# Conv row factors from fp32 sums beside the last input units, the samples' cast queued behind the second key block's, and another order of the last units

## The chip, the cores and the metric

The kernel runs on one core of one Trainium2 chip. The metric is the device time of one execution in microseconds; the time of a kernel is the median of several executions. Engines are named as the profile names them: PE (TensorE, matrix products; PEld its weight loads), DVE (VectorE), ACT (ScalarE), POOL (GpSimd) and SP (SyncE, which here issues the DMAs).

## What is computed

One streaming step of one hybrid layer, for 512 frames of a new stream (the prompt) and 64 frames of a running one (the samples, with 512 cached frames). D is 2048, there are 8 heads of 128, 1024 conv channels in 8 groups, and an FFN of width 5632.

```python
hn = rmsnorm(x, g_norm1)
q, k, v, gb, gc, hc = split(hn @ w_in)              # six blocks of 1024 columns
q = rmsnorm(q, g_q); k = rmsnorm(k, g_k)            # per head
o_attn = stick_breaking_blocks(q, k_all, v_all)     # keys and values: cached + new
u = gc * hc
o_conv = gb * conv3_causal(u)                       # three taps, state from conv_past
mix = concat([rmsnorm(o_attn, g_attn_out), rmsnorm(o_conv, g_conv_out)])   # each over its 1024 channels
x = x + mix @ w_out
h2 = rmsnorm(x, g_norm2)
x = x + (silu(h2 @ w_gate) * (h2 @ w_up)) @ w_down
```

In stick-breaking attention the weight of key s for query t is beta_ts times the product of (1 - beta_tj) over the keys j between them, beta being the sigmoid of the scaled score. Outputs are the new x of both streams, the new key and value rows, and the conv states.

## The kernel before

**Layout.** Frames lie along the free axis: 576 columns (512 prompt frames, then 64 sample frames), handled as two halves of 288 (`HALVES`). Channels lie on the 128 partitions. A product in high precision is made of three fp32r matmuls: an operand is split into a high part (an ACT cast to fp32r) and a low part (a DVE subtraction), and hi·hi, lo·hi and hi·lo are added up in PSUM. `split()` (L230 to L232) does one such split; `whl` tiles hold the split weights.

**Units.** The input projection runs in 22 units (`HEADS_A`, numbered -22 to -1), each two blocks of 128 columns by two halves of frames, made by seven products (1 to 7, a Strassen-like scheme) in place of eight. The last three are -3 (a pair of `gb` groups), -2 (q and k of head 7) and -1 (v of heads 6 and 7). `order` lists all products `(unit, product)`; `run()` issues one, 24 matmuls in eight steps with a `pipe.tick()` behind each. Behind product number k_, `prepare()` splits the operand of number k_ + 4. Products 1, 6, 5 and 3 of a unit add to one bank (`psy`), 7 and 4 to another (`psw`); `kept()` copies psy into a one-buffer tile (tags "ms", "t", "acc") between them, since several results are made of more than one product. `a_done()` finishes a quarter of a unit: for q and k it multiplies by the row factor R1 of the first norm, squares, splits the squares (`s2`) and spawns `normed()`.

**Pipeline.** `Pipeline` is a queue of generators on a count of ticks. What a generator issues between two yields stands in program order at the tick at which it came due; `yield n` puts it off by n ticks, and `spawn(gen, delay)` starts it. `normed()` sums the squares over the partitions with `channel_sums()` (two matmuls with a matrix of ones, into one of two PSUM banks of tag "misc"), forms 1/sqrt with Ln, Exp and a Newton step, and scales q or k. `tokens()` transposes a block on PE (also into "misc" banks) and stores its rows.

**Orders.** PE runs in program order (it is scheduled by hand). For the other engines and the DMA queue, the order of the stage around the change is laid out by a planner at compile time, which takes ready instructions by program order. Each engine then runs its own order and waits on semaphores.

**Conv group and output projection.** A `gb` unit leaves the conv half of `mix` (without its row factor) in `mixc_dram`, and adds the squares to `accc`. Behind the last unit, `group_scale(accc, Rc)` splits the sums of squares, adds them over the partitions with `channel_sums()`, and turns them into row factors `Rc` by `rsqrt_mean()`. `out_proj()` multiplies the conv half by `w_out`, 16 column blocks by two halves of frames; a DVE step (L1005) scales each bank by the row factor and another (L1006) adds it to x.

**Heads.** `heads()` spawns `attend(h)` every 29 ticks, so that the eight heads run beside the conv half's projection. `attend` makes the scores of three query-key groups z2, z1, z0 and of the samples (`zs`), softplus of each, then, by sums with triangular matrices on PE, the exponents; `weights(b)` masks (L1135, DVE), exponentiates (L1137, ACT) and splits (`ph`, `pl`). `po` (L1170, L1173) is the product with the values. For the samples, `sp` (softplus) gets running sums on POOL (L1113 to L1117), `split(sph, spl, sp)` splits it, and `sample_weights()` (L1125 to L1131) uses it later, between the first and the second key block of `po`. The squares of the attention output are added to `accA`, and at the start of the second `out_proj()` the same `group_scale()` gives `Ra`. Then come the FFN's units.

Of the kernel before, what the change touches and what calls it, by code (L numbers as in the profile page):

```python
# [10 lines left out]
F32 = mybir.dt.float32  # L11
F32R = mybir.dt.float32r
AF = mybir.ActivationFunctionType
ALU = mybir.AluOpType
PSUM = bass.MemoryType.PSUM

P = 128
TP = 512
TS = 64
T = TP + TS  # L20
HALF = T // 2
HALVES = ((0, HALF), (HALF, T))
# [79 lines left out]
def tile_hybrid_stream_step(  # L102
# [6 lines left out]
    nc = tc.nc  # L109
    mm = nc.tensor.matmul  # L110
# [5 lines left out]
    kp, vp, ks, vs = k_prompt[0, 0], v_prompt[0, 0], k_sample[0, 0], v_sample[0, 0]  # L116
# [6 lines left out]
    rpool = ctx.enter_context(tc.tile_pool(name="rpool", bufs=1, side="left"))  # L123
    tmp = tc.alloc_tile_pool(name="tmpa", bufs=2, side="left")
# [15 lines left out]
    def misc(name):  # L140
        return ps_z.tile([P, 512], F32, tag="misc", name=name, bufs=2)
# [42 lines left out]
    def load_weight():  # L184
        i = len(raws)
        raws[i], raw3, src = weight_raw(i)
        nc.sync.dma_start(out=raw3, in_=src)
# [33 lines left out]
    pipe = Pipeline()  # L221
# [6 lines left out]
            pipe.tick()  # L228

    def split(hi, lo, src, lo_eng=None):  # L230
        nc.scalar.copy(out=hi, in_=src)  # L231
        (lo_eng or nc.vector).tensor_tensor(out=lo, in0=src, in1=hi.bitcast(F32), op=ALU.subtract)  # L232

    def parts(name, bufs=2):
        t = tmp.tile([P, 2, HALF], F32R, tag="hl", name=name, bufs=bufs)
# [5 lines left out]
    oner = const.tile([P, P], F32R, name="oner")  # L241
# [24 lines left out]
    epsc = const.tile([P, 1], F32, name="epsc")  # L266
# [5 lines left out]
    def rsqrt_mean(dst, src, n, width):  # L272
        ms = tmp.tile([P, HALF], F32, tag="ms", name="ms", bufs=1)[:, :width]
        y = tmp.tile([P, HALF], F32, tag="acc", name="y", bufs=1)[:, :width]
        t = tmp.tile([P, HALF], F32, tag="t", name="t", bufs=1)[:, :width]
        nc.vector.tensor_scalar(out=ms, in0=src, scalar1=1.0 / n, scalar2=EPS, op0=ALU.mult, op1=ALU.add)
        nc.scalar.activation(out=y, in_=ms, func=AF.Ln)
        nc.scalar.activation(out=y, in_=y, func=AF.Exp, scale=-0.5)
        nc.vector.tensor_tensor(out=t, in0=y, in1=y, op=ALU.mult)
        nc.vector.scalar_tensor_tensor(out=t, in0=t, scalar=-0.5, in1=ms, op0=ALU.mult, op1=ALU.mult)  # L280
        nc.vector.scalar_tensor_tensor(out=dst, in0=t, scalar=1.5, in1=y, op0=ALU.add, op1=ALU.mult)

    def channel_sums(src_hi, src_lo, a, b, name):
        ps = misc(name)[:, : b - a]
        mm(ps, oner, src_hi, start=True, stop=False)
        mm(ps, oner, src_lo, start=False, stop=True)
        return ps
# [466 lines left out]
    def tokens(E, dst, dst_s, dram, lag):  # L754
        yield lag
        pa = misc("tok_a")
        for i in range(4):
            nc.tensor.transpose(pa[:, i * P : (i + 1) * P], E[:, i * P : (i + 1) * P], ident)
        ta = hl_tile("tok")[:, :TP]
        nc.scalar.copy(out=ta, in_=pa)  # L760
        ta = ta.rearrange("p (i d) -> p i d", d=P)
        nc.sync.dma_start(out=dst.rearrange("(i p) d -> p i d", p=P), in_=ta)
        if dram is not None:
            nc.sync.dma_start(out=dram[:, :4, :], in_=ta)
        yield 3
        pb = misc("tok_b")
        nc.tensor.transpose(pb[:, :P], E[:, T - P : T], ident)
        tb = hl_tile("tokz")[:, :P]
        nc.scalar.copy(out=tb, in_=pb[:, :P])
        nc.sync.dma_start(out=dst_s, in_=tb[TS:, :])  # L770
        if dram is not None:
            nc.sync.dma_start(out=dram[:, 4, :], in_=tb)
# [3 lines left out]
    accc = []  # L776
# [3 lines left out]
        return ((a, min(b, TP), 0),) + (((TP, b, 2),) if b > TP else ())  # L780

    def normed(n, h, c, a, b, s2, E):
        yield 17
        ms = ss = channel_sums(s2[:, 0], s2[:, 1], a, b, "ss")
        yt = hl_tile("yt")
        y, t = yt[:, :HALF], yt[:, HALF:]
        nc.scalar.activation(out=ms, in_=ss, func=AF.Identity, scale=1.0 / P, bias=epsc)
        nc.scalar.activation(out=y, in_=ms, func=AF.Ln)
        nc.scalar.activation(out=y, in_=y, func=AF.Exp, scale=-0.5)
        nc.scalar.activation(out=t, in_=y, func=AF.Square)  # L790
        nc.vector.scalar_tensor_tensor(out=t, in0=t, scalar=-0.5, in1=ms, op0=ALU.mult, op1=ALU.mult)
        nc.vector.scalar_tensor_tensor(out=t, in0=t, scalar=1.5, in1=y, op0=ALU.add, op1=ALU.mult)
        nc.vector.scalar_tensor_tensor(out=E[:, a:b], in0=E[:, a:b], scalar=col("gk") if c else gqs, in1=t,
                                       op0=ALU.mult, op1=ALU.mult)
        seen[n, c] = seen.get((n, c), 0) + 1
        if seen[n, c] == 2:
            nc.sync.dma_start(out=qk_dram[h, c], in_=E)
            if c:
                pipe.spawn(tokens(E, kp[:, h, :], ks[:, h, :], None, 8 if n == -2 else 20))

    def a_finish(n, c, i, ps, part):
        if UNITS[n][0] == "gb" and c == i == 0:
# [106 lines left out]
             (2 - NA, 5)]  # L909
    for n in range(2 - NA, -3):  # L910
        order += [(n + 1, 1), (n, 3), (n, 4), (n + 1, 2), (n + 1, 6), (n + 1, 7), (n + 1, 5)]
    order += [(-2, 1), (-3, 3), (-3, 4), (-2, 2), (-2, 6), (-2, 5), (-1, 1), (-2, 3), (-1, 2), (-2, 7),
              (-2, 4), (-1, 3), (-1, 6), (-1, 5), (-1, 7), (-1, 4)]
    early = {-NA, 1 - NA, -1}
    mixc = []
    for k_ in range(2, 4):
        prepare(*order[k_])
    for k_, (n, p_) in enumerate(order):
        run(n, p_, n in early)
        if k_ + 4 < len(order):  # L920
            prepare(*order[k_ + 4])
            if order[k_ + 4] in ((-2, 3), (-1, 6)):
                load_weight()
        if (n, p_) == (-1, 3):
            xpool.release()
            cpool = tc.alloc_tile_pool(name="cpool", bufs=1, reuse_waits="tile", side="right")
            mixc = cpool.tile([P, NG, 2, T], F32R, name="mixc")
            for g in range(NG):
                nc.sync.dma_start(out=mixc[:, g].bitcast(F32), in_=mixc_dram[g])
        if (n, p_) == (-1, 7):  # L930
            split_weight(nc.vector)
# [56 lines left out]
    mixa = []  # L988
# [7 lines left out]
    def out_proj(frame, R, after=None):  # L996
        for c in range(D // 256):
            whi, wlo = next_weight()
            load_x2()
            for j in range(2):  # L1000
                kt = 2 * c + j
                for a, b in HALVES:
                    ps = ps_pj.tile([P, HALF], F32, tag="pj", name="pjo")
                    product(ps, whi, wlo, slice(j * P, (j + 1) * P), frame, 8, a, b)
                    nc.vector.tensor_tensor(out=ps, in0=ps, in1=R[:, a:b], op=ALU.mult)  # L1005
                    nc.vector.tensor_tensor(out=x2(kt)[:, a:b], in0=ps, in1=x2(kt)[:, a:b], op=ALU.add)  # L1006
                if after:
                    after(kt)

    Rc = rpool.tile([P, T], F32, tag="R", name="Rc", bufs=2)  # L1010

    def group_scale(acc_, R, bufs):
        p_ = []
        for a, b in HALVES:
            s2 = tmp.tile([P, 2, HALF], F32R, tag="hl", name="s2g", bufs=bufs)
            split(s2[:, 0], s2[:, 1], acc_[:, a:b])
            p_.append(s2)
        yield 4
        for s2, (a, b) in zip(p_, HALVES):
            ss = channel_sums(s2[:, 0], s2[:, 1], a, b, "ssg")  # L1020
            rsqrt_mean(R[:, a:b], ss, 8 * P, HALF)

    def state_out():
        yield 9
# [45 lines left out]
    def attend(h):  # L1070
# [45 lines left out]
        for b in (2, 1, 0):  # L1116
            nc.gpsimd.tensor_tensor(out=sums[:, b * TS : (b + 1) * TS], in0=sums[:, (b + 1) * TS : (b + 2) * TS],  # L1117
                                    in1=sp[:, (b + 1) * TS : (b + 2) * TS], op=ALU.add)
        split(sph, spl, sp)
        yield 8  # L1120
        if h + 1 < NH:
            keys_cached(h + 1)
# [10 lines left out]
        def weights(b):  # L1133
            for i in ((2, 3) if b == 2 else (b,)):
                nc.vector.scalar_tensor_tensor(out=zb[i][:, :P], in0=zb[i][:, :P], scalar=0.0, in1=mneg,  # L1135
                                               op0=ALU.min, op1=ALU.add)
            nc.scalar.activation(out=pr[b][:, : full[b]], in_=z[b][:, : full[b]], func=AF.Exp)  # L1137
            split(ph[b], pl[b], pr[b][:, : width[b]])

        yield 3  # L1140
        mm(zb[3], trif, pb[3], stop=False, **kw)
# [6 lines left out]
        mm(zb[1], trir, pl[1], stop=False, **kw)  # L1148
        mm(zb[1][:, P:], neg1r, s1h, stop=False, **kw)
        mm(zb[1][:, P:], neg1r, s1l, stop=True, **kw)  # L1150
        weights(1)
        yield 4
        mm(zb[0], trir, ph[0], stop=False, **kw)
        mm(zb[0], trir, pl[0], stop=False, **kw)
# [50 lines left out]
            pipe.spawn(attend(h))  # L1205
            yield PERIOD

    pipe.spawn(group_scale(accc[0], Rc, 3))
    pipe.spawn(state_out())
    pipe.spawn(heads())  # L1210
    out_proj(lambda k: (mixc[:, k, 0, :], mixc[:, k, 1, :]), Rc)
    pipe.flush()
    accA = bt["accA"]
    cpool.release()
# [2 lines left out]
    tmp = tc.alloc_tile_pool(name="tmp", bufs=2, reuse_waits="tile", side="left")  # L1217
    lpad = tc.alloc_tile_pool(name="lpad", bufs=1, side="left")
    lpad.tile([P, 64], F32, name="lpad_t")
    Ra = rpool.tile([P, T], F32, tag="R", name="Ra", bufs=2)  # L1220
    pipe.spawn(group_scale(accA, Ra, 2))

# [34 lines left out]
            for k in (4 * m, 4 * m + 2):  # L1259
                nc.sync.dma_start(out=x2_dram[k : k + 2].rearrange("k p t -> p k t"), in_=x2t[k // 2])  # L1260

    out_proj(lambda k: mixa[k], Ra, after_b2)
    R2 = rpool.tile([P, T], F32, tag="R", name="R2", bufs=2)
    parts2 = []
    for i in range(2):
# [340 lines left out]
```

## Time and profile before

| | us |
|---|---|
| median of 3 runs (lowest, highest) | 2406.14 (2406.02, 2406.74) |
| the profiled execution | 2408.49 |
| its span, first to last instruction | 2406.8 |
| PE busy | 2355.5 |
| DVE busy | 1939.7 |
| ACT busy | 1235.0 |
| POOL busy | 298.9 |
| input units | up to about 598 of the span |
| conv projection with the heads | about 598 to 799 |
| attention projection, FFN | from about 799 |

How to read the lines: a row of the timeline has the start, the duration, engine, source line, operation, output<-inputs, shapes and a count, and in brackets the idle time of the engine before it and what ended that. A row of the waits has who waited for whom, the total, the times and the longest. A row of the windows has the stretch and its length, then the busy time (and instructions) of PE, PEld, DVE, ACT and POOL in it, the granted clock of PE, the DMA share and GB/s.

### The profile page before, as it was taken

Reading aid. Unit: us, or ns where it says so; the run is one execution under the profiler, and the core shown is the slowest. Engines: PE = TensorE matmul, PEld = TensorE weight load, DVE = VectorE, ACT = ScalarE, POOL = GpSimd, SP = SyncE. Lnnn points to the kernel's source line nnn. Section 1 sums busy time; section 2 is a strip of 40 time slices with the busy share of each in tenths; the row PEclk is TensorE's granted clock in tenths of the full one; section 3 lists DMA queues with packets and bytes.
Section 4 is the critical chain, followed back from the end, with each engine's and each line's share of the span. In section 5 each row is a group of like instructions: output and inputs, shape, how many; then the busy total and the mean of one; then the engine's idle time right before and its main releaser. Section 6 shows DMA issues by size and latency. Waiting matters only on the chain.

```text
span 2406.8 us, 43812 instructions
## 1 busy us (share of the span) xinstructions
PE 2355.5 (98%) x17609; PEld 2339.5 (97%) x17609; DVE 1939.7 (81%) x2840; ACT 1235.0 (51%) x2207; POOL 298.9 (12%) x377
## 2 busy tenths in 40 slices
PE   8899999999999999999999999999999899999998
PEld 8899999998889999999999999999999899999998
DVE  7888898797677768888888888888888778887875
ACT  7456656455677545444444444444444444444454
POOL 0111121120233222000000000000000002431211
PEclk9999999999999999999999999999999999999999
DMA  7433342535632233535444444444444936885642
GB/s 253 140 113 108 108 140 86 161 99 184 224 107 89 100 127 118 155 112 158 150 128 145 146 143 132 144 150 141 129 152 141 339 112 205 221 226 195 205 128 79
DMA packets 474900, 360.60 MB, mean 150 GB/s; under 512 B 11278, under 2 KB 460680, under 8 KB 474696
## 3 DMA queue, kind: packets, MB, share of 16 engines
q1 hardware_dynamic: 469528, 351.02, 45.7%
q0 software_dynamic: 5168, 6.79, 1.6%
q8 instruction: 138, 2.26, 0.4%
q14 instruction: 66, 0.54, 0.1%
HBM read 281.39 MB, written 76.37 MB: 149 GB/s over the span
## 4 chain that ended last, share of the span: by engine, by line
PE 82%; DVE 6%; ACT 4%; issue 2%; POOL 2%; DMA 1%; SPq 0%; ACTq 0%; DVEq 0%; POOLq 0%
PE psy L405 43%; PE psw L405 21%; PE psx L405 10%; PE pjo L227 5%; DVE whl L232 1%; ACT whl L231 1%; PE pw L1388 1%; ACT ph L231 0%; PE psv L405 0%; PE pot L1511 0%; DVE c L866 0%; DVE raw_b L349 0%; POOL hbl L1117 0%; DMA raw_a<-in_w_down_dram 0%; DVE wlo L180 0%
## 5 line engine op out<-in xcount | busy, mean ns | idle before, releaser
L232 DVE TENSOR_TENSOR whl<-raw_a,whl 128x1024 fp32r<-128x1024 f32 (+4 forms) x376 | 426.4, 1135 | 69.4 <-ACT whl L231 67.8
L405 PE MATMUL psy<-t,whl 128*128 128x288 f32 x2916 | 438.4, 295 | 0.5 <-ACT part L428 0.5
L231 ACT CAST whl<-raw_a 128x1024 fp32r<-128x1024 f32 (+4 forms) x376 | 352.6, 938 | 137.9 <-PE psx L405 47.8
L405 PE MATMUL psy<-h_s,whl 128*128 128x288 f32 x2724 | 411.7, 295 | 6.8 <-ACT part L428 6.8
L405 PEld LDWEIGHTS psy<-t,whl 128*128 128x128 f32 x2916 | 403.7, 189 | 0.9 <-ACT part L428 0.7
L405 PEld LDWEIGHTS psy<-h_s,whl 128*128 128x128 f32 x2724 | 378.5, 189 | 7.3 <-ACT part L428 7.3
L405 PE MATMUL psw<-t,whl 128*128 128x288 f32 x2592 | 377.1, 295 | 0.0
L405 PEld LDWEIGHTS psw<-t,whl 128*128 128x128 f32 x2592 | 354.4, 189 | 0.2
L232 DVE TENSOR_TENSOR whl<-raw_b,whl 128x1024 fp32r<-128x1024 f32 (+5 forms) x230 | 248.7, 1081 | 86.4 <-ACT whl L231 85.1
L231 ACT CAST whl<-raw_b 128x1024 fp32r<-128x1024 f32 (+5 forms) x230 | 207.6, 904 | 206.9 <-PE psw L405 70.8
L428 ACT COPY part<-psy 128x288 f32<-128x288 f32 x303 | 121.2, 400 | 348.5 <-PE psy L405 346.4
L405 PE MATMUL psx<-h_s,whl 128*128 128x288 f32 x1122 | 165.1, 295 | 2.7 <-DVE gs L1368 2.7
L405 PEld LDWEIGHTS psx<-h_s,whl 128*128 128x128 f32 x1122 | 154.1, 188 | 2.9 <-issue 2.9
L231 ACT CAST whl<-s 128x1024 fp32r<-128x1024 f32 (+5 forms) x101 | 93.4, 924 | 119.9 <-PE psw L405 112.3
L405 PE MATMUL psy<-t12a,whl 128*128 128x288 f32 x1056 | 150.5, 295 | 3.1 <-ACT part L428 3.1
L405 PE MATMUL psw<-t34a,whl 128*128 128x288 f32 x1056 | 150.4, 295 | 2.1 <-DVE ghs L854 0.9
L405 PEld LDWEIGHTS psy<-t12a,whl 128*128 128x128 f32 x1056 | 143.5, 188 | 4.0 <-ACT part L428 4.0
L405 PEld LDWEIGHTS psw<-t34a,whl 128*128 128x128 f32 x1056 | 143.2, 188 | 2.7 <-DVE ghs L854 1.1
L227 PE MATMUL pjo<-mixc,whi 128*128 128x288 f32 x512 | 123.0, 307 | 1.2 <-ACT kcT L1063 1.2
L232 DVE TENSOR_TENSOR whl<-s,whl 128x1024 fp32r<-128x1024 f32 (+5 forms) x101 | 107.5, 1064 | 19.6 <-ACT whl L231 18.0
L1331 POOL DMA_DIRECT2D hid_dram<-form x3 | 2.4, 809 | 921.1 <-DVE form L232 921.1
L227 PE MATMUL pjo<-mixa,whi 128*128 128x288 f32 x512 | 102.1, 295 | 0.0
(599 smaller groups left out, 4146.8 us busy)
## 6 DMA issues: line engine op xcount, KB each, us to landing
hid_dram<-form SPq DMA_DIRECT2D x147, 288.0 KB, 2.3
raw_a<-in_w_gate_dram SPq DMA_DIRECT2D x23, 1024.0 KB, 6.2
raw_a<-in_w_up_dram SPq DMA_DIRECT2D x23, 1024.0 KB, 5.5
raw_a<-in_w_in_dram SPq DMA_DIRECT2D x22, 1024.0 KB, 5.5
raw_b<-in_w_in_dram SPq DMA_DIRECT2D x22, 1024.0 KB, 7.9
raw_b<-in_w_gate_dram SPq DMA_DIRECT2D x21, 1024.0 KB, 6.6
raw_b<-in_w_up_dram SPq DMA_DIRECT2D x21, 1024.0 KB, 7.7
h_s<-hid_dram SPq DMA_DIRECT2D x10, 2016.0 KB, 9.2
```

What stands on the lines that cost most here:

```text
L227: mm(ps, w_[:, k, csl], x_[:, a:b], start=(k == 0 and n == 0), stop=(k == nk - 1 and n == 2))
L231: nc.scalar.copy(out=hi, in_=src)
L232: (lo_eng or nc.vector).tensor_tensor(out=lo, in0=src, in1=hi.bitcast(F32), op=ALU.subtract)
L405: mm(ps, whl[:, w_, j, :], x_, start=(start and j == 0 and q == 0), stop=(j == len(xs_) - 1 and q == 2), skip_group_check=True)
L428: nc.scalar.copy(out=t, in_=st["y"])
L1331: q.dma_start(out=hid_dram[fp][2 * n - 2 : 2 * n].rearrange("f p t -> p f t"), in_=t.bitcast(F32))
L1388: mm(pss[j, i], w_[:, k, j * P : (j + 1) * P], x_, start=(kk == 0 and k == 0 and n == 0), stop=(kk == 1 and k == 7 and n == 2))
```

## The change

Four things are changed.

1. `group_scale()` no longer splits the sums of squares. It adds them over the partitions with one fp32 matmul a half, works in place in the PSUM bank and in a tile of tag "hl", and writes the row factors over the sums (`accc`, `accA`), so that `Rc` and `Ra` are gone. One half is done per tick.
2. For the conv half it is spawned behind product (-2, 6) with a delay of 5 ticks, in place of behind the last unit; for the attention half, with a delay of 4.
3. In the order of the last products, (-1, 1) and (-1, 2) come earlier, and (-2, 4) later. For unit -2, `normed()` waits 12 ticks and not 17, and `tokens()` of its keys 5 and not 8. The loads tied to places in the order go with them: two of `w_out`, and those of `mixc` behind (-1, 3).
4. The split of the samples' softplus is traced behind `weights(1)`, and its cast is put behind that call's cast in ACT's order (`tc.issue_after`).

```diff
     def split(hi, lo, src, lo_eng=None):
-        nc.scalar.copy(out=hi, in_=src)
+        cast = nc.scalar.copy(out=hi, in_=src)
         (lo_eng or nc.vector).tensor_tensor(out=lo, in0=src, in1=hi.bitcast(F32), op=ALU.subtract)
+        return cast.ins
...
     def normed(n, h, c, a, b, s2, E):
-        yield 17
+        yield 12 if n == -2 else 17
...
-                pipe.spawn(tokens(E, kp[:, h, :], ks[:, h, :], None, 8 if n == -2 else 20))
+                pipe.spawn(tokens(E, kp[:, h, :], ks[:, h, :], None, 5 if n == -2 else 20))
+
+    def group_scale(acc_, bufs):
+        for a, b in HALVES:
+            ss = misc("ssg")[:, :HALF]
+            mm(ss, oner.bitcast(F32), acc_[:, a:b], start=True, stop=True)
+            yt = tmp.tile([P, 2, HALF], F32, tag="hl", name="ytg", bufs=bufs)
+            y, t = yt[:, 0], yt[:, 1]
+            nc.scalar.activation(out=ss, in_=ss, func=AF.Identity, scale=1.0 / (8 * P), bias=epsc)
+            nc.scalar.activation(out=y, in_=ss, func=AF.Ln)
+            nc.scalar.activation(out=y, in_=y, func=AF.Exp, scale=-0.5)
+            nc.scalar.activation(out=t, in_=y, func=AF.Square)
+            nc.vector.scalar_tensor_tensor(out=t, in0=t, scalar=-0.5, in1=ss, op0=ALU.mult, op1=ALU.mult)
+            nc.vector.scalar_tensor_tensor(out=acc_[:, a:b], in0=t, scalar=1.5, in1=y, op0=ALU.add, op1=ALU.mult)
+            yield 1
...
-    order += [(-2, 1), (-3, 3), (-3, 4), (-2, 2), (-2, 6), (-2, 5), (-1, 1), (-2, 3), (-1, 2), (-2, 7),
-              (-2, 4), (-1, 3), (-1, 6), (-1, 5), (-1, 7), (-1, 4)]
+    order += [(-2, 1), (-3, 3), (-3, 4), (-2, 2), (-2, 6), (-1, 1), (-2, 5), (-1, 2), (-2, 3), (-2, 7), (-1, 3),
+              (-1, 6), (-2, 4), (-1, 5), (-1, 7), (-1, 4)]
...
+        if (n, p_) == (-2, 6):
+            pipe.spawn(group_scale(accc[0], 3), 5)
...
-    Rc = rpool.tile([P, T], F32, tag="R", name="Rc", bufs=2)
-
-    def group_scale(acc_, R, bufs):
-        p_ = []
-        for a, b in HALVES:
-            s2 = tmp.tile([P, 2, HALF], F32R, tag="hl", name="s2g", bufs=bufs)
-            split(s2[:, 0], s2[:, 1], acc_[:, a:b])
-            p_.append(s2)
-        yield 4
-        for s2, (a, b) in zip(p_, HALVES):
-            ss = channel_sums(s2[:, 0], s2[:, 1], a, b, "ssg")
-            rsqrt_mean(R[:, a:b], ss, 8 * P, HALF)
...
-        split(sph, spl, sp)
         yield 8
...
-            split(ph[b], pl[b], pr[b][:, : width[b]])
+            return split(ph[b], pl[b], pr[b][:, : width[b]])
...
-        weights(1)
+        behind = weights(1)
+        with tc.issue_after(behind):
+            split(sph, spl, sp)
...
-    pipe.spawn(group_scale(accc[0], Rc, 3))
...
-    out_proj(lambda k: (mixc[:, k, 0, :], mixc[:, k, 1, :]), Rc)
+    out_proj(lambda k: (mixc[:, k, 0, :], mixc[:, k, 1, :]), accc[0])
...
-    pipe.spawn(group_scale(accA, Ra, 2))
+    pipe.spawn(group_scale(accA, 2), 4)
...
-    out_proj(lambda k: mixa[k], Ra, after_b2)
+    out_proj(lambda k: mixa[k], accA, after_b2)
```

More of the change, by code (lines that the diff above doesn't have):

```diff
@@ L1219, in tile_hybrid_stream_step @@
     lpad.tile([P, 64], F32, name="lpad_t")
-    Ra = rpool.tile([P, T], F32, tag="R", name="Ra", bufs=2)
-    pipe.spawn(group_scale(accA, Ra, 2))
+    pipe.spawn(group_scale(accA, 2), 4)
     h2pool = tc.alloc_tile_pool(name="h2pool", bufs=1, reuse_waits="tile", side="left")
```

## The prediction

> **What bounds the kernel now.** I read the page first, then the busy time by stage, then what PE waited for, and last the order of time around each wait.
>
> ```profile
> span 2406.8 us, 43812 instructions
> PE 2355.5 (98%) x17609; PEld 2339.5 (97%) x17609; DVE 1939.7 (81%) x2840; ACT 1235.0 (51%) x2207; POOL 298.9 (12%) x377
> 549.77:598.13 48.36, 44.75 (x332) 43.61 (x330) 33.46 (x49) 26.13 (x46) 1.78 (x3) 1.00 0.51 183
> 598.13:609.56 11.43, 8.44 (x49) 7.53 (x47) 9.03 (x22) 6.74 (x16) 1.47 (x2) 0.85 0.65 203
> 609.56:799.07 189.51, 178.40 (x1247) 170.85 (x1246) 131.76 (x283) 135.05 (x307) 55.63 (x104) 0.97 0.39 129
> ```
>
> PE is the bound: 2355.5 of 2406.8 us. The three windows are the stages that the diff touches: the last twelve products of the input units, the start of the conv half's output projection, and the eight attention heads beside it. In them PE stands idle 3.61, 2.99 and 11.11 us, 17.7 together, and in two the granted clock is below 1 (0.85, 0.97). So the change can move little more than these waits and the slow stretches behind them; shorter work on DVE or ACT counts only where PE waits for it. PE runs in program order; the other engines' orders come from a planner, so they may shift.
>
> ```profile
> PE po L1170 <- ACT pr L1137: 5.3, 4, 2.5
> PE z L1147 <- ACT ph L231: 2.5, 1, 2.5
> PE pjo L227 <- ACT kcT L1063: 1.2, 1, 1.2
> ACT sph L231 <- POOL hbl L1117: 16.6, 8, 2.9
> ```
>
> Among the heads, PE waits above all for the exponentials of L1137, and ACT itself stands 16.6 us in front of one cast, the samples' sph, until POOL has its sums.
>
> **The change part by part.** Gains carry a minus.
>
> *(a) The last input units.* One product and the waits:
>
> ```profile
> 549.64 3.33 PE L405 MATMUL psx<-bod,whl 128*128 128x288 f32 x24
> 552.81 3.33 PE L405 MATMUL psy<-t12a,whl 128*128 128x288 f32 x24
> 557.78 3.47 PE L405 MATMUL psy<-t12a,whl 128*128 128x288 f32 x24 [1.63 <-ACT part L428]
> 574.88 1.05 PE L405 MATMUL psw<-t34a,whl 128*128 128x288 f32 x6 [0.64 <-DVE E L820]
> 585.74 1.06 PE L405 MATMUL psy<-t12a,whl 128*128 128x288 f32 x6 [0.49 <-ACT part L428]
> ```
>
> Start to start a product takes 3.17 us: eight ticks of 0.40, 0.13 a matmul. The three waits are products that add to a bank directly behind the one that wrote it: (-2,5) behind (-2,6), (-2,4) behind (-2,7), (-1,5) behind (-1,6). The new order puts another product between each pair, which covers 3.17 us, so these go: -2.76. The operands are still prepared four places ahead.
>
> But the new order makes a wait. (-1,6) now comes before (-2,4). Both units keep their second sum in the tag "t", which has one buffer, and (-2,4) is the last reader of unit -2's. So the copy of (-1,6) must wait for (-2,4) and its DVE sum, and (-1,5), the next product, waits for the copy. The price is a DVE sum and an ACT copy in a row, 0.64 + 0.49 = 1.13 by the two rows above, up to 2.0 if a queue is busy: +1.3. On ACT the casts of later operands may queue behind that copy; they are due four products later.
>
> The conv scale's sums come to stand here, as two fp32 matmuls. Those of the trace with 128 columns:
>
> ```profile
> 711.94 0.38 PE L1141 MATMUL z<-pr,trir 128*128 128x128 f32 x2
> 712.15 0.39 PE L1142 MATMUL z<-pr,neg1r 128*128 128x128 f32 x2
> ```
>
> 0.21 us for 128 columns; for 288 between 0.21 (if the weights bound it) and 0.47 by the columns. I take 0.47, as these are streams of columns: +0.94 for two.
>
> Where they stand matters more. normed() of (-2,2) now waits 12 ticks, and group_scale is spawned behind (-2,6) with 5: both come due on the same tick of (-1,1), normed first. Each sum takes one of the two "misc" banks, and the ACT steps work in place, so a bank is held up to the DVE step that reads it last:
>
> ```profile
> 561.88 0.29 PE L285 MATMUL ss<-s,oner 128*128 128x288 f32 x1
> 558.05 0.46 DVE L828 TENSOR_TENSOR s<-psx,s 128x288 fp32r<-128x288 f32 x1
> 564.58 0.45 DVE L791 SCALAR_TENSOR_TENSOR yt<-yt,ss 128x288 f32<-128x288 f32 x1 [0.69 <-ACT yt L790]
> ```
>
> A bank is held from 561.88 to 565.03, 3.15 us. One tick later the second half of group_scale wants a third bank. PE is back for it after two sums (0.26), one fp32 sum (0.47) and three matmuls (0.40), 1.13 us: it waits 2.0, or up to 3.0 if ACT mixes the two chains. I take 2.3. Ahead of that normed itself comes 13 ticks behind (-2,2), which ended at 552.8: near 558.0, before DVE has ended its operand at 558.51: +0.5. All of PE stands still behind these waits. group_scale's eight ACT and four DVE steps, each like the 0.45 of L791, lie beside products; DVE is busy 33.46 of 48.36 us in this window and ACT 26.13, so I give them nothing.
>
> Such an idle stretch may also cost clock:
>
> ```profile
> 557.72:561.13 3.41, 3.35 (x25) 3.35 (x26) 2.89 (x4) 1.25 (x3) 0.00 (x0) 1.00 0.93 304
> 786.42:789.83 3.41, 2.03 (x12) 1.44 (x12) 3.19 (x8) 1.64 (x5) 0.00 (x0) 1.00 0.00 0
> 789.83:793.25 3.42, 3.42 (x15) 3.42 (x14) 1.84 (x5) 1.66 (x3) 0.00 (x0) 0.50 0.28 64
> 721.57:724.98 3.41, 3.41 (x16) 3.13 (x15) 1.50 (x5) 1.64 (x3) 0.00 (x0) 0.50 0.00 0
> 605.51:608.92 3.41, 3.41 (x17) 3.31 (x16) 2.72 (x6) 1.58 (x6) 0.00 (x0) 0.50 0.90 280
> ```
>
> After 1.38 us idle (786.42 to 789.83) the clock fell to 0.50 for 3.4 us, while behind the 1.63 us wait it stayed at 1.00. A half-speed stretch loses 1.7 us. With the case open I take half: +0.8. The Trainium skill, TensorE: Matmul & The Clock Gate, in "Why this matters for your kernels", says that gaps up to some 3 us do no harm; by that these 0.8 us would fall away. The trace does not agree: 1.38 us were enough.
>
> Last, unit -2's key tokens: normed's sum to the transpose took
>
> ```profile
> 586.63 0.29 PE L285 MATMUL ss<-s,oner 128*128 128x288 f32 x1
> 590.56 0.66 PE L758 MATMUL tok_a<-ident,E 128*128 128x128 f32 x4 [0.30 <-DVE E L793]
> ```
>
> 3.93 us, the last 0.30 a wait, at a lag of 8 ticks. With 5 ticks PE is there 1.2 us sooner and the chain is no shorter; a token transpose of unit -1 in between hides some: +1.0 (0 to 1.2).
>
> The stores of these tokens move three products later on SP, the eight mixc loads and the second w_out load one product earlier, the first w_out load one later; each has over 10 us until its use, so I give them nothing. (a) is -2.76 + 1.3 + 0.94 + 2.3 + 0.5 + 0.8 + 1.0 = +4.1, bounds -1 to +7.
>
> *(b) Start of the conv projection.* What leaves:
>
> ```profile
> 601.06 0.40 PE L285 MATMUL ssg<-s2g,oner 128*128 128x288 f32 x1 [0.60 <-ACT s2g L231]
> 603.17 0.40 PE L286 MATMUL ssg<-s2g,oner 128*128 128x288 f32 x1 [1.71 <-DVE s2g L232]
> ```
>
> With a third that is not shown the 2.99 us of idle time of this window, four sums of 0.13 (0.5), and the half-speed stretch from 605.51 (1.7): -5.2. Casts, subtractions and Ln/Exp leave ACT and DVE here.
>
> *(c) Head 0.* Without (b) PE reaches the first scores (609.56) about 5 us sooner. They need kf and its two parts:
>
> ```profile
> 601.88 0.42 SPq L954 DMA_DIRECT2D kf<-qk_dram  x1
> 606.56 0.69 DVE L232 TENSOR_TENSOR kl<-kf,kh 128x512 fp32r<-128x512 f32 x1
> ```
>
> kl ended at 607.25, PE would come at 604.4. If SP issues kf where it did, PE waits 2.9 us; if the later tokens let it go ahead, nothing. +1.2. The wait at L1147 (2.5) hangs on ACT's order in head 0; I leave it.
>
> *(d) Heads 1 to 7, the samples' cast.* One head in order of time:
>
> ```profile
> 712.50 0.28 PE L1144 MATMUL z<-hbe,trir 128*128 128x256 f32 x1
> 715.71 0.74 DVE L232 TENSOR_TENSOR kl<-kf,kh 128x512 fp32r<-128x512 f32 x1
> 717.46 0.67 ACT L231 CAST sph<-hbl 128x576 fp32r<-128x576 f32 x1 [2.39 <-POOL hbl L1117]
> 718.17 0.76 DVE L232 TENSOR_TENSOR spl<-hbl,sph 128x576 fp32r<-128x576 f32 x1 [1.72 <-ACT sph L231]
> 719.21 0.69 DVE L1135 SCALAR_TENSOR_TENSOR z<-z,mneg 128x128 f32<-128x128 f32 x3
> 719.73 0.49 ACT L1137 ACTIVATE hbl<-z 128x384 f32<-128x384 f32 x1 [1.60 <-DVE z L1135]
> 720.89 0.42 ACT L231 CAST hbe<-pr 128x256 fp32r<-128x256 f32 x1
> 720.66 0.49 PE L1170 MATMUL po<-pr,vtok 128*128 128x128 f32 x2 [2.51 <-ACT pr L1137]
> 723.09 0.47 PE L1125 MATMUL zs<-sph,trir 128*128 128x320 f32 x1
> ```
>
> PE ended the scores' sums of z2 at 712.78, but their mask (L1135) ran at 719.21, because spl stood ahead of it on DVE and waited for sph, and sph on ACT for POOL. Queued behind weights(1)'s cast, sph cannot come ahead of the masks either: that cast needs them, so the planner must put spl behind them on DVE too. The mask can then start when kl ends, 716.45, the exponentials near 716.9, and po, which PE reached at 718.15, waits no more. The waits 5.3 and 1.2 (kcT stood behind the same cast) go, and with them the half-speed stretches of 721.57 and 789.83: -9.9.
>
> Behind the cast now stands the samples' product. Mask 0.46, four ACT steps 1.58 (719.73 to 721.31), sph 0.67, spl 0.76: spl ends at 719.9. PE came to L1125 2.43 us behind po, of which the half clock from 721.57 on made 0.76; with 1.67 it comes at 719.8 and waits 0.1 us. What follows sph on ACT, weights(0)'s exponential, is due later than that. Other heads will lie on either side: I take 0.2 in each of seven, +1.5 (0 to 7). (d) is -8.4.
>
> *(e) The attention half's scale.* Two fp32 sums for four fp32r sums, 0.94 - 0.52: +0.4. PE did not wait there.
>
> The sum is 4.1 - 5.2 + 1.2 - 8.4 + 0.4 = -7.9 us. The profiled execution took 2408.49 us (its span 2406.8); the median of the three timed runs is 2406.14, 2.35 less, and the difference is taken from that: **2398.2 us**.
>
> **The rivals.**
> *The wait moves to the samples' product.* ACT's exponentials may come out later than I have them, and spl with them; then each of seven heads waits some 1 us at L1125, without a slow stretch. For it: in the one head that I followed the margin is already -0.1 us. Against: there kl held DVE up to 716.45, and a head in which DVE is free sooner has room. (d) becomes -9.9 + 7.0 = -2.9, the sum -2.4: 2403.7.
> *Slower: masks late on DVE.* The whole chain mask, exponential, cast, sph, spl now hangs on the moment at which DVE takes L1135, and DVE has long runs of weight work:
>
> ```profile
> 701.60 2.49 DVE L180 TENSOR_TENSOR wlo<-raw_a,whi 128x512 fp32r<-128x512 f32 x4
> ```
>
> If such a run (2.49 us) stands ahead of L1135 in most heads, PE waits 1.8 us at L1125 in eight heads, 14.4, with four slow stretches, 6.8: (d) is +11.3, the sum +11.8: 2417.9. It passes the time of before by 4.8 us from about 1 us a head on. Against it: DVE stood idle 1.72 us in front of spl, time that the masks can have.
> *Head 0 comes free too.* Without group_scale's buffers of tag "hl" the open_b tiles can be had sooner, z1's exponentials move ahead in ACT's order, and the wait at L1147 (2.5), its slow stretch (1.7) and my 1.2 for kf go: -13.3, 2392.8. Against it: PE comes sooner too, and (c) may as well make this wait longer.
>
> **How the numbers follow.** A measurement of this kernel can tell about 0.2%, 4.8 us, from no change. My forecast has 0.52 and head 0 coming free 0.10: both faster by more than that. The wait that moves has 0.25: within 0.2%. Late masks have 0.13: slower. The range, 2391 to 2409, takes in the first three with their bounds ((a) alone spans 8 us) and leaves out the last; the forecast alone is 2393 to 2402.
>
> **What would show it.** In the changed profile: no ssg wait behind 598; a wait of 2 to 3 us at an ssg sum inside (-1,1), and some 1.3 us at (-1,5) for ACT's part copy; no wait of ACT at sph for POOL near 16.6 us; L1170's waits for L1137 gone; granted clock 1.00 among heads 1 to 7. I am wrong if L1125 shows waits above 1 us in most heads, or if the tail of the input units loses over 7 us.

## The result, and the profile after

| | us |
|---|---|
| before, median of 6 runs | 2406.63 (2406.02 to 2407.16) |
| changed kernel, median of 6 runs | 2397.88 (2394.20 to 2399.21) |
| ratio, 95% interval | 0.9961 (0.9950 to 0.9972) |
| profiled execution, before and after | 2408.49, 2397.15 |

The change makes the kernel 8.8 us (0.4%) faster. The two profiled executions are 11.3 us apart. The page of the changed kernel begins:

```profile
span 2395.4 us, 43789 instructions
PE 2350.2 (98%) x17609; PEld 2336.2 (98%) x17609; DVE 1934.0 (81%) x2828; ACT 1234.6 (52%) x2211; POOL 300.3 (13%) x377
```

The windows are cut at six marks of PE's program order: the start of (-2,2), the first matmul of the conv projection, the first scores of head 0, those of head 1, the first matmul of the attention projection, and the first of the FFN. First the kernel before, then the changed one (stretch, length, busy PE, PEld, DVE, ACT, POOL, granted clock, DMA share, GB/s):

```profile
549.64:598.13 48.49, 44.88 (x333) 43.74 (x331) 33.59 (x49) 26.13 (x46) 1.78 (x3) 1.00 0.51 182
...
609.56:632.83 23.27, 20.67 (x141) 19.75 (x140) 14.09 (x33) 14.97 (x33) 5.43 (x11) 0.93 0.97 337
632.83:799.07 166.24, 157.74 (x1108) 151.10 (x1107) 117.67 (x251) 120.08 (x275) 50.20 (x93) 0.98 0.31 99
799.07:952.83 153.76, 153.76 (x1162) 153.76 (x1161) 114.37 (x216) 78.06 (x160) 33.10 (x38) 1.00 0.35 114
952.83:2406.80 1453.97, 1436.68 (x10850) 1434.38 (x10848) 1183.93 (x1624) 666.08 (x1097) 119.44 (x130) 1.00 0.51 160
```

```profile
549.26:599.38 50.12, 45.47 (x337) 44.35 (x336) 35.17 (x55) 28.64 (x55) 2.28 (x5) 1.00 0.50 177
599.38:604.94 5.56, 5.56 (x44) 5.37 (x43) 4.81 (x10) 4.22 (x9) 0.45 (x1) 1.00 0.78 206
604.94:629.71 24.77, 19.95 (x142) 18.43 (x141) 14.75 (x34) 16.22 (x34) 5.45 (x11) 1.00 1.02 363
629.71:783.96 154.25, 152.07 (x1107) 147.46 (x1106) 116.76 (x248) 119.00 (x273) 52.37 (x93) 1.00 0.34 107
783.96:938.18 154.22, 154.22 (x1162) 154.01 (x1161) 112.25 (x210) 78.95 (x163) 33.24 (x39) 1.00 0.34 114
938.18:2395.40 1457.22, 1439.94 (x10850) 1437.63 (x10848) 1183.50 (x1624) 665.05 (x1097) 119.15 (x130) 0.99 0.51 160
```

By length: the tail of the input units +1.6 us, the start of the conv projection 5.9 less (11.43 before, in the prediction's window), head 0 +1.5, heads 1 to 7 12.0 less, the attention projection +0.5, the FFN +3.3, and 0.4 less ahead of all this. Nearly all that is gained is gained in heads 1 to 7. What PE waited for from the tail to the end of the heads:

```profile
PE kc L1066 <- DMA cK<-in_cache_k_dram: 2.5, 1, 2.5
PE zs L1129 <- DVE spl L232: 2.3, 6, 0.6
PE ssg L805 <- DVE yt L792: 2.2, 1, 2.2
PE z L1150 <- ACT ph L231: 1.1, 1, 1.1
PE psy L406 <- ACT part L429: 1.0, 1, 1.0
PE tok_a L759 <- DVE neg1r L980: 0.9, 1, 0.9
```

The waits for L1137 (now L1140) are gone; in their place stand the samples' product (L1129), the third bank (L805), the one buffer of "t" (L406), the token transpose, and a load made in head 0, that of the cached keys of head 1 (`keys_cached(h + 1)`, L1066). ACT's own wait in front of sph fell from 16.6 us to this:

```profile
ACT sph L231 <- POOL hbl L1121: 0.3, 1, 0.3
```

### The profile page after: what moved, and what is told of

The parts are those of the page before. It is cut to its first block, busy times and chain, and to the rows that moved or that the text cites. A ratio compares the mean times of both kernels' runs of the same rounds, so it can differ in the third digit from the quotient of the medians.

```text
span 2395.4 us, 43789 instructions
## 1 busy us (share of the span) xinstructions
PE 2350.2 (98%) x17609; PEld 2336.2 (98%) x17609; DVE 1934.0 (81%) x2828; ACT 1234.6 (52%) x2211; POOL 300.3 (13%) x377
## 4 chain that ended last, share of the span: by engine, by line
PE 82%; DVE 6%; ACT 4%; issue 2%; DMA 1%; POOL 1%; SPq 0%; DVEq 0%; ACTq 0%; POOLq 0%
PE psy L406 43%; PE psw L406 21%; PE psx L406 10%; PE pjo L227 5%; DVE whl L232 1%; DMA v_dram<-tok 1%; PE pw L1391 1%; ACT whl L231 1%; ACT ph L231 0%; PE pot L1514 0%; DVE c L881 0%; ACT whi L179 0%; DMA raw_a<-in_w_down_dram 0%; DVE raw_b L350 0%; DVE wlo L180 0%
## 5 line engine op out<-in xcount | busy, mean ns | idle before, releaser
L406 PE MATMUL psy<-t,whl 128*128 128x288 f32 x2916 | 437.3, 295 | 0.5 <-ACT part L429 0.5
L406 PE MATMUL psy<-h_s,whl 128*128 128x288 f32 x2724 | 411.8, 295 | 6.8 <-ACT part L429 6.8
L406 PEld LDWEIGHTS psy<-t,whl 128*128 128x128 f32 x2916 | 403.4, 189 | 0.9 <-ACT part L429 0.7
L406 PEld LDWEIGHTS psy<-h_s,whl 128*128 128x128 f32 x2724 | 378.7, 189 | 7.3 <-ACT part L429 7.3
L406 PE MATMUL psw<-t,whl 128*128 128x288 f32 x2592 | 377.2, 295 | 0.0
L406 PEld LDWEIGHTS psw<-t,whl 128*128 128x128 f32 x2592 | 354.0, 189 | 0.2
L406 PE MATMUL psx<-h_s,whl 128*128 128x288 f32 x1122 | 166.8, 297 | 2.7 <-DVE gs L1371 2.7
L406 PEld LDWEIGHTS psx<-h_s,whl 128*128 128x128 f32 x1122 | 156.2, 191 | 2.9 <-issue 2.9
L406 PE MATMUL psy<-t12a,whl 128*128 128x288 f32 x1056 | 150.0, 295 | 2.0 <-ACT part L429 2.0
L406 PE MATMUL psw<-t34a,whl 128*128 128x288 f32 x1056 | 150.4, 295 | 1.4 <-DVE ghs L869 0.9
L406 PEld LDWEIGHTS psy<-t12a,whl 128*128 128x128 f32 x1056 | 143.2, 188 | 2.7 <-ACT part L429 2.7
L406 PEld LDWEIGHTS psw<-t34a,whl 128*128 128x128 f32 x1056 | 143.4, 188 | 1.9 <-DVE ghs L869 1.1
```

What stands on the lines that cost most here:

```text
L406: mm(ps, whl[:, w_, j, :], x_, start=(start and j == 0 and q == 0), stop=(j == len(xs_) - 1 and q == 2), skip_group_check=True)
```

## The experiments

My theory: the cast brings most of the gain; the scale's move and the new order win at the start of the projection, and lose part of it to three new waits in the tail and to head 0. The rival: the scale and the order bring the gain, and the heads only profit from a better start. Times of single stages are of the one profiled execution of each kernel; each median stands beside the kernel before in the same job (2408.49 for e1 to e4, 2408.08 for e5 to e8, 2406.64 for e9 and e10). The ratios are not the quotients of these medians; they differ from them by up to 0.0011.

**e1: the cast alone, on the kernel before.**

```diff
-        split(sph, spl, sp)
         yield 8
...
-        weights(1)
+        behind = weights(1)
+        with tc.issue_after(behind):
+            split(sph, spl, sp)
```

> The kernel before with the fourth part of the change alone: the samples' split behind weights(1). Theory: most of the gain is here. Heads 1 to 7 should lose their waits at L1170 for the exponentials and both slow stretches of the clock, 10 to 12 us, the last input units and the start of the conv projection stay as before (48.5 and 11.4 us), head 0 stays at some 23 us: 2394 to 2397. Rival (the gain comes from the group scale and the order of the last units, the heads only profit from a better start): 2402 to 2406, with waits left at L1170.

2395.70 us, ratio 0.9958 (0.9943 to 0.9973): no slower than the whole change (its profiled FFN, unlike that of the changed kernel, has no slow stretch, which is worth some 3 us; more on this below). The windows of the tail and of heads 1 to 7, and all that PE waited for in these heads:

```profile
549.68:598.04 48.36, 44.76 (x332) 43.63 (x331) 33.57 (x49) 26.10 (x46) 1.78 (x3) 1.00 0.51 181
632.58:786.60 154.02, 151.94 (x1108) 147.57 (x1107) 117.10 (x249) 119.29 (x274) 52.05 (x93) 1.00 0.34 107
PE zs L1126 <- DVE spl L232: 2.3, 5, 0.6
```

The tail is that of before, heads 1 to 7 lose 12.2 us (166.24 to 154.02). The rival falls: by ratio, the cast alone does as much as the whole change (0.9961).

**e2: the changed kernel without the cast.** The same edit undone.

```diff
+        split(sph, spl, sp)
         yield 8
...
-        behind = weights(1)
-        with tc.issue_after(behind):
-            split(sph, spl, sp)
+        weights(1)
```

> The changed kernel without its fourth part: the samples' split is back ahead of the 8 ticks. Theory: the tail of the input units stays at some 50.1 us and the start at 5.6 (together 4.2 us less than before), heads 1 to 7 go back to 166 us with waits at L1170 and at least one slow stretch: 2401 to 2405. Rival: the heads stay near 155 us and the time near 2398.

2406.41 us, ratio 0.9997 (0.9987 to 1.0007): no change from before, 1.4 us over the top of what I expected. Heads 1 to 7 are back at 165 us, with the waits for the exponentials:

```profile
550.01:601.76 51.75, 47.10 (x336) 45.81 (x335) 35.16 (x55) 28.74 (x55) 2.28 (x4) 0.97 0.49 172
631.72:796.74 165.02, 157.06 (x1107) 151.03 (x1106) 117.43 (x251) 119.74 (x275) 49.67 (x93) 0.98 0.32 101
PE po L1174 <- ACT pr L1141: 5.5, 5, 2.5
```

The tail is 1.6 us longer than in the changed kernel, though its PE order and its waits are the same; its clock is 0.97. This is the half-speed stretch behind the bank's wait that the prediction left open. The stretch with the wait and the one after it, first of e2, then of the changed kernel:

```profile
558.50:561.90 3.40, 1.22 (x8) 0.88 (x7) 3.37 (x5) 3.11 (x9) 0.00 (x0) 0.99 0.13 27
561.90:565.30 3.40, 3.40 (x12) 3.12 (x13) 1.53 (x4) 1.59 (x6) 0.00 (x0) 0.50 0.84 279
```

```profile
557.72:561.10 3.38, 1.19 (x9) 0.85 (x7) 3.35 (x5) 3.10 (x9) 0.00 (x0) 1.00 0.11 18
561.10:564.50 3.40, 3.40 (x24) 3.29 (x25) 1.69 (x5) 2.68 (x7) 0.00 (x0) 1.00 0.90 288
```

The same idle time, 2.2 us each, once with and once without the slow clock; the last section tells what differs.

**e3: the scale alone, on the kernel before.** The new `group_scale()` behind (-2,6), with the old order and the old lags (17 and 8).

```diff
-    pipe.spawn(group_scale(accc[0], Rc, 3))
...
+        if (n, p_) == (-2, 6):
+            pipe.spawn(group_scale(accc[0], 3), 5)
```

> The kernel before with the new group scale at its new place, with the old order of the last units and the old lags of 17 and 8 ticks, and without the samples' cast. Here normed comes 5 or more ticks away from the group scale, so no third bank is wanted at once. Theory: the tail grows only by the two fp32 sums (0.3 each by the changed kernel's trace) and stays at some 49 us, with the old waits of 1.6, 0.6 and 0.5; the start of the conv projection falls from 11.4 to some 5.6 us; heads as before: 2399 to 2402. Rival (the wait for a bank belongs to the fp32 sums, wherever they stand): tail 51 us, 2402 to 2404.

2407.85 us, ratio 1.0003 (0.9994 to 1.0012): theory and rival both failed, this part alone gains nothing. Tail, start and head 0, with the waits that are new there:

```profile
549.17:599.17 50.00, 46.02 (x337) 44.44 (x336) 35.11 (x53) 28.90 (x54) 1.78 (x3) 1.00 0.50 177
599.17:606.79 7.62, 5.71 (x44) 5.29 (x42) 5.09 (x13) 4.49 (x10) 1.46 (x2) 1.00 0.49 144
606.79:632.25 25.46, 21.68 (x139) 20.18 (x140) 13.53 (x30) 14.74 (x32) 5.45 (x11) 0.93 1.02 351
PE kc L1065 <- DMA cK<-in_cache_k_dram: 2.1, 1, 2.1
PE z L1084 <- ACT kh L231: 1.9, 1, 1.9
```

The wait for a bank is small here (0.4 us, at a sum of `normed()`), so it does hang on `normed()` coming due on the same tick. The tail grows by 1.5 (two sums at 0.49 us each, for the 0.3 expected, and this wait), the start falls by 3.8 and not by 5.9, since PE now waits 1.9 us at its end for kh; head 0 grows by 2.2 through the wait for the cached keys of head 1, which are loaded there. These three make -0.1; the attention projection adds its 0.5.

**e4: three waits of the tail taken away**, on the changed kernel.

```diff
-        st["u2"] = kept("ms" if n == NGU - 1 else "t")
+        st["u2"] = kept("ms" if n in (NGU - 1, -1) else "t")
...
     def group_scale(acc_, bufs):
...
-            yield 1
+            yield 8
...
-                pipe.spawn(tokens(E, kp[:, h, :], ks[:, h, :], None, 5 if n == -2 else 20))
+                pipe.spawn(tokens(E, kp[:, h, :], ks[:, h, :], None, 8 if n == -2 else 20))
```

> The changed kernel with three waits of its tail taken away at their cause: the copy of (-1,6) goes to the tag ms, which is free by then; the second half of the group scale comes 8 ticks behind the first; the key tokens of unit -2 wait 8 ticks again. Theory: the waits of 0.98 (ACT's copy), 2.19 (third bank) and most of 0.93 (token transpose) go, the tail falls from 50.1 to 46 to 46.5 us, and the time by up to 4 us, 2393 to 2395, unless head 0 gives it back. Rival (head 0 waits for its loads, which hang on the last value tokens and not on PE): PE comes 4 us sooner and waits 4 us longer at head 0's cached keys; the time stays at 2397 to 2399.

2390.05 us, ratio 0.9934 (0.9919 to 0.9949), below what theory and rival had. The tail falls by 4.9 us to 45.21, more than expected, with only the 0.55 at (-1,4) left of its waits; some of that is the key tokens, which have slid behind its end. The start gives 1.65 back. That is 3.3 us net; of the 6.8 us between the two profiled executions (2397.15 and 2390.31) 3.2 lie in the FFN, where e4 has no slow stretch, and so are not the edits' own by anything that I can show:

```profile
548.52:593.73 45.21, 44.66 (x336) 44.22 (x335) 34.99 (x53) 28.08 (x54) 1.99 (x3) 1.00 0.53 190
593.73:600.94 7.21, 5.68 (x45) 5.37 (x42) 5.10 (x13) 4.69 (x10) 1.47 (x2) 1.00 0.67 185
PE kc L1066 <- DMA cK<-in_cache_k_dram: 2.4, 1, 2.4
PE z L1085 <- ACT kh L231: 1.5, 1, 1.5
```

**e5: the tag alone**, the first of e4's three edits, on the changed kernel.

```diff
-        st["u2"] = kept("ms" if n == NGU - 1 else "t")
+        st["u2"] = kept("ms" if n in (NGU - 1, -1) else "t")
```

> The changed kernel with one tag changed: ACT's copy for (-1,6) goes to ms in place of t. Theory (the wait of 0.98 ahead of (-1,5) comes from the one buffer of tag t): that wait is gone, the other waits of the tail (2.2 for the third bank, 0.9 at the token transpose, 0.55 at (-1,4)) stay, the tail falls by 1.0 us to 49.1. Rival (ACT is simply late there): 0.5 us or more are left.

2392.99 us (one run). The wait at (-1,5) is gone, those of 2.2, 0.95 and 0.55 stay, the tail is 48.9 us: 1.2 less than in the changed kernel. The wait came from the one buffer. Head 0 took most of it back: the wait for the cached keys is 3.3 us in place of 2.5.

**e6: the new order alone, on the kernel before.**

```diff
-    order += [(-2, 1), (-3, 3), (-3, 4), (-2, 2), (-2, 6), (-2, 5), (-1, 1), (-2, 3), (-1, 2), (-2, 7),
-              (-2, 4), (-1, 3), (-1, 6), (-1, 5), (-1, 7), (-1, 4)]
+    order += [(-2, 1), (-3, 3), (-3, 4), (-2, 2), (-2, 6), (-1, 1), (-2, 5), (-1, 2), (-2, 3), (-2, 7), (-1, 3),
+              (-1, 6), (-2, 4), (-1, 5), (-1, 7), (-1, 4)]
```

> The kernel before with the new order of the last products alone; old lags of 17 and 8 ticks, old group scale, no cast moved. Theory: the waits of 1.63, 0.64 and 0.49 go and one of 1.0 at (-1,5) comes; the tail falls from 48.5 to about 46.8 us; the old wait of 3 us at the group scale and its slow stretch stay at the start (11.4 us); 2405 to 2407. Rival (the order gains nothing: the waits only change places): tail 48 to 49 us.

2405.31 us (one run). The tail falls to 45.4 us, 3.1 less, of which a token transpose that has moved behind its end is a part; the three old waits are gone and one of 1.3 stands at (-1,5). The start grows by 1.1 to 12.5, and not as I had expected: its slow stretch is gone (granted clock 1.00) and 0.7 us are left of the wait at the group scale's sums, but PE waits 3.0 us for kh.

**e7: one x tile later**, on e4: one `load_x2()` fewer ahead of the projection.

```diff
-    load_x2()
```

> The kernel of e4 with one of the two x tiles that are loaded ahead of the projection loaded one column block later. Theory (head 0 waits because 590 KB of x stand ahead of its value and cached key loads in the one DMA queue): the wait for the cached keys falls from 2.4 to under 1 us and its slow stretch goes; the wait for kh (1.5), whose load is issued earlier, stays; 2386 to 2389. Rival (that load hangs on PE's transpose of the keys before it, or on the value tokens' stores): 2.4 us stay, time as e4, 2390.

2390.51 us against 2390.05 for e4: no gain. The cached keys' wait is 1.9 us in place of 2.4, the slow stretch stays. So x's 590 KB are not what holds that load, or at most for 0.5 us.

**e8: the cached keys through POOL's queue**, on e4.

```diff
-        nc.sync.dma_start(out=cK, in_=ck[:, h, :].rearrange("(i p) d -> p i d", p=P))
+        nc.gpsimd.dma_start(out=cK, in_=ck[:, h, :].rearrange("(i p) d -> p i d", p=P))
```

> The kernel of e4 with the cached keys loaded through POOL's queue and not SP's. Theory (the load is late because SP issues it behind stores and loads that wait): the wait at head 0 goes below 1 us, 2386 to 2389. Rival (the DMA engines are full there, so another queue changes nothing, and POOL's own issue time delays its sums): 2390 to 2394, with new waits of ACT for POOL in the heads.

2393.69 us, ratio 0.9949 (0.9932 to 0.9965): no gain, and 3.6 us above e4's median, though the intervals of the two overlap. The wait for the keys is gone, but PE waits 3.7 us a few us later, at L1150, for ACT's ph (none over 0.15 in e4), and 2.0 for kh. The new waits of ACT for POOL, which the rival wanted, are not there: from 594 to 780 they come to 12.4 us, against 13.0 in e4.

**e9: the last unit's value tokens stored through POOL's queue**, on e4.

```diff
+        q = nc.gpsimd if lag == 3 else nc.sync
         yield lag
...
-        nc.sync.dma_start(out=dst.rearrange("(i p) d -> p i d", p=P), in_=ta)
+        q.dma_start(out=dst.rearrange("(i p) d -> p i d", p=P), in_=ta)
```

(and so with its three other stores)

> The kernel of e4 with the stores of the last unit's value tokens (four a head, two heads) issued by POOL and not by SP. Theory (in e4 head 0 waits 1.9 us for the parts of kf and 2.4 for the cached keys because SP stands in these stores ahead of their loads): both waits fall below 0.5 us, the slow stretch at head 0 goes, 2385 to 2387. Rival (the transfers themselves are slow there, all 16 DMA engines being full): both waits stay within 1 us of what they were, 2389 to 2392.

2388.43 us, ratio 0.9926 (0.9908 to 0.9944), the lowest median of all, though its interval overlaps that of e4. The wait for the cached keys is gone; that for kh has grown to 3.2:

```profile
592.83:601.72 8.89, 5.69 (x44) 5.38 (x42) 5.56 (x14) 4.50 (x10) 3.84 (x6) 1.00 1.01 330
601.72:624.67 22.95, 21.46 (x140) 20.09 (x140) 14.96 (x32) 15.98 (x34) 6.24 (x11) 0.93 0.90 315
PE z L1086 <- ACT kh L231: 3.2, 1, 3.2
```

Neither theory has both sides: SP's queue held the keys (2.4 to none: in e4 SP issued head 1's keys at 610.16, 4.4 us behind PE's last use of the buffer, in e9 at 608.09, at once), but qf and kf, issued 1.7 us sooner, landed no sooner, in a stretch with a DMA share of 1.01. The Trainium skill, DMA: Bandwidth & Descriptors, in "Issuing engines are not separate DMA queues", has it that queues of different engines share the same 16 DMA engines, so that another queue saves issue time only. e9 agrees with both halves of this.

**e10: e4 without the scale's move** (the old `group_scale()` at its old place, the old lags).

```diff
-        if (n, p_) == (-2, 6):
-            pipe.spawn(group_scale(accc[0], 3), 5)
...
+    pipe.spawn(group_scale(accc[0], Rc, 3))
```

> The kernel before with the new order (the copy of (-1,6) in tag ms), and with the samples' cast behind the second key block's, but with the old group scale at its old place and the old lags. Set against e4, it prices the move of the group scale. Theory (the move saves the 3 us of waits and the slow stretch at the start, and head 0 gives about half of it back): tail 44 to 45 us, start 11 to 13, heads 177 to 179, time 2392 to 2395, 2 to 5 us above e4. Rival (head 0 gives all of it back): within 1 us of e4, 2390.

2392.34 us, ratio 0.9943 (0.9927 to 0.9959), 2.3 above e4's median and within what was expected; the intervals of the two overlap, so that the gain of the move is not shown by the times. Its stages by length are 43.8, 12.1, 22.9 and 154.1 us (tail, start, head 0, heads 1 to 7); e4's are 45.2, 7.2, 25.1 and 154.2. So of the 4.9 us that the move saves at the start, 1.4 go in the tail and 2.2 in head 0, 0.4 in the attention projection and 0.1 in heads 1 to 7: 0.7 net by the stages. So head 0 gives back about half, as the theory had it, but with the tail's part hardly anything of the move is left.

## Why the prediction was right

It said 2398.2 us and 2397.88 came, by way of the forecast and not of a rival. That the two lie 0.3 us apart is luck. By stages the profiled executions differ by -11.4 us (of span) and not by -7.9: (a) cost 2.5 us less than forecast, (b) and (c) gained 0.4 more and (d) 3.6 more, 0.4 came ahead of the tail, and the FFN lost 3.3 that I did not have. And the medians are 2.5 us closer together than the profiled executions (8.8 and 11.3).

**(a), the tail: +4.1 forecast, +1.6 measured.** The three old waits are gone, and the new ones stand where they were forecast:

```profile
561.09 0.75 PE L805 MATMUL ssg<-accc,oner 128*128 128x288 f32 x2 [2.19 <-DVE yt L792]
586.39 3.48 PE L406 MATMUL psy<-t12a,whl 128*128 128x288 f32 x24 [0.98 <-ACT part L429]
596.41 0.63 PE L759 MATMUL tok_a<-ident,E 128*128 128x128 f32 x4 [0.93 <-DVE neg1r L980]
```

2.19 for 2.3 at the third bank, 0.98 for 1.3 at tag "t", and a transpose wait of 0.93 where 0.30 stood, +0.6 for +1.0. e5 and e4 take them away at their causes. Two terms did not come: the 0.5 in front of normed (the subtraction that ended at 558.51 before ended at 557.28 now, since DVE's order was laid out anew), and the 0.8 for the clock, which was half of a coin: 0 here, 1.6 in e2. With the smaller waits these make 2.1 of the 2.5 us; 0.4 I cannot place.

**(b) and (c), start and head 0: -4.0 forecast, -4.4 measured.** The start lost its waits and its slow stretch, 5.9 us for 5.2. In head 0, +1.5 for +1.2 is luck: the wait that I put at kf (0 to 2.9) did not come, and another one did, of 2.5 us, for the cached keys of head 1. Their load overwrites head 0's keys, which PE had used by 609.24; SP issued it only at 613.83, behind the value tokens' stores and the loads of head 0's values:

```profile
613.83 0.38 SPq L976 DMA_DIRECT2D cK<-in_cache_k_dram  x1
617.17 0.63 PE L1066 MATMUL kc<-ident,cK 128*128 128x128 f32 x4 [2.54 <-DMA cK<-in_cache_k_dram]
```

Against it, the wait at L1147 (2.5, now L1150) fell to 1.1 and its slow stretch went, which I had only in a rival. In e3, e4 and e6 to e10 PE does wait for kh, 1.4 to 3.2 us. Head 0 gives back part of what is gained ahead of it.

**(d), the cast: -8.4 forecast, -12.0 measured.** The step that was mis-sized is the list of what leaves: I had the waits for L1137 and kcT and two slow stretches, 9.9 us. PE's idle time in heads 1 to 7 fell from 8.50 to 2.18 us, 6.3, and the two stretches make 3.4. Against the forecast, the small waits for hbe at po went too (2.0 us, all but 0.2), and the new waits at L1129, 1.9 us of the 2.3 above in these heads, were as forecast (1.5). The remaining 2.3 us left PE's busy time, not its idle time, and sat beside the waits. Counted from the start of one matmul to the start of the next, and without idle time and slow clock, PE takes 4.3 us less around `po`'s first products (L1170 and the hbe ones of L1173), where the waits went, and 2.0 us more at the samples' product (now L1128 and L1129), where the new ones stand: a wait costs more than the idle time that the profile gives it. One head in order of time, to be set beside the one of before:

```profile
709.15 0.82 DVE L1138 SCALAR_TENSOR_TENSOR z<-z,mneg 128x128 f32<-128x128 f32 x3
709.87 0.49 ACT L1140 ACTIVATE pr<-z 128x384 f32<-128x384 f32 x1 [2.36 <-DVE z L1138]
711.33 0.68 ACT L231 CAST sph<-hbl 128x576 fp32r<-128x576 f32 x1
712.24 0.75 DVE L232 TENSOR_TENSOR spl<-hbl,sph 128x576 fp32r<-128x576 f32 x1
```

The mask is ahead of spl on DVE, as it must be; sph follows 1.5 us behind the first exponential.

**(e): +0.4 forecast, +0.46 measured.** Two fp32 sums for four others; the rows are under the last heading.

**Not forecast: the FFN, +3.3 us.** Its code and its waits are the same. Behind a wait of 2.7 us near its start the clock fell in the changed kernel, and stayed in the kernel before:

```profile
949.76:953.17 3.41, 2.65 (x11) 2.68 (x12) 3.41 (x5) 2.12 (x4) 0.79 (x1) 0.50 0.41 143
953.17:956.59 3.42, 3.42 (x16) 3.42 (x15) 1.86 (x3) 0.00 (x0) 0.00 (x0) 0.50 0.24 86
```

```profile
965.40:968.80 3.40, 3.40 (x27) 3.40 (x27) 3.40 (x5) 2.02 (x5) 0.22 (x1) 1.00 0.27 94
```

Of the rivals, the wait did move to the samples' product, but at 0.2 to 0.6 us in five of the seven heads and not 1; the masks cost PE nothing, though ACT now waits 17.4 us for them (L1140 for L1138) in place of 8.9; head 0 did not come free as a whole.

## What to carry to other kernels

A cast that waits for a slow engine holds everything behind it in its engine's order: put it behind the work that is ready, even if its own user then waits a little (12 us here for one cast a head). When such a queue of waits is shortened, look at what is loaded next: of each us saved ahead of head 0, part came back there. An earlier place for a step is only free if its banks and its one-buffer tiles are free at that place too; here a `yield`, a lag and a tag took 3.3 us net out of the tail and the start, beside the 4.2 that the move and the new order had brought there (5.87 less 1.63). What is left of such gains has to be read from the whole: with parts 1 to 3 of the change alone (e2) the time stayed where it was.

## What the runs showed of the hardware

The fall of the clock behind a wait is not fixed by the wait's length. The same 2.2 us at the third bank cost a half-speed stretch in e2 and none in the changed kernel and e5; the same 2.7 us in the FFN were followed by none (before, e1, e3, e4, e6, e9, e10), one (e2, e5, e8) or two (the changed kernel, e7) stretches of 3.4 us, and the FFN took 1452.8 to 1454.1, 1455.0 to 1455.2 and 1456.4 to 1457.2 us.

What differs is how the wait lies on a grid of time. In each of the twelve profiles all slow stretches start whole multiples of 3.413 us apart; in the kernel before, those at 605.51, 625.99, 721.57 and 789.83 are 6, 28 and 20 such steps apart. The grid lies elsewhere in each execution. Counted back from the slow stretches, the 2.18 us at the third bank lie within one step in e2, and are cut into 1.74 and 0.45 in the changed kernel and into 1.57 and 0.60 in e5. Of the FFN's wait (2.66 to 2.69 us in all twelve), the longest part in one step was 1.37 to 1.80 us where the clock stayed, and 1.90 to 2.50 where it fell. The steps that hold that part, and the next ones, in e3 (idle 1.80) and in the changed kernel (idle 1.90; the next one is shown above):

```profile
963.58:966.99 3.41, 1.61 (x12) 1.65 (x13) 3.41 (x5) 2.16 (x5) 0.80 (x1) 1.00 0.51 180
966.99:970.40 3.41, 3.41 (x28) 3.41 (x28) 3.41 (x6) 1.54 (x3) 0.00 (x0) 1.00 0.22 80
```

```profile
946.35:949.76 3.41, 1.51 (x12) 1.28 (x10) 3.38 (x5) 2.33 (x3) 0.00 (x0) 1.00 0.34 124
```

A second slow stretch followed where the wait ran on for 0.74 or 0.76 us into the first. Idle time in a step is not the whole of it, though: 1.38 us were enough in a head of the kernel before, and 1.91 at head 1's keys in the changed kernel were not.

The Trainium skill, TensorE: Matmul & The Clock Gate, in "What's actually happening", calls the window in which activity is counted free-running; these runs agree with that, and not with the other section of the page that the prediction quoted.

The fp32 sum of 288 columns hands PE on after 0.27 us, but the matmul behind it then holds PE 0.35 us and not 0.13:

```profile
785.54 0.65 PE L805 MATMUL ssg<-accA,oner 128*128 128x288 f32 x2
785.81 0.51 PE L227 MATMUL pjo<-mixa,whi 128*128 128x288 f32 x1
786.16 0.30 PE L227 MATMUL pjo<-mixa,wlo 128*128 128x288 f32 x1
```

With the 0.13 taken off that this matmul needs anyway, a sum costs 0.49 us, as priced from the columns (0.47).
